# A segment mean on one core: the order of the first probe pieces and data tiles, the sizes and lead of the later pieces, and the place of the last block's counts

## The chip, the core and the metric

The kernel runs on one core of a Trainium2 chip. The core has five engines with instruction queues of their own: PE (TensorE), DVE (VectorE), ACT (ScalarE), POOL (GpSimd) and SP (SyncE, which here only issues transfers). Sixteen DMA engines move the data. The metric is the device time of one execution in microseconds (us); less is better.

## The reference

Ten million floats come with sorted segment numbers from 0 to 9999; the result is the mean of each segment.

```python
def reference(data, segment_ids):
    num_segments = int(segment_ids.max()) + 1
    sums = np.zeros(num_segments, dtype=np.float32)
    counts = np.zeros(num_segments, dtype=np.float32)
    np.add.at(sums, segment_ids, data)
    np.add.at(counts, segment_ids, 1)
    return sums / np.maximum(counts, 1)
```

The ids are drawn at random and then sorted, so a segment has about 1000 elements.

## The kernel before

Each of the 128 partitions holds 78,125 elements in a row. They are cut into 90 rows of L = 875 (the last row is shorter: 250). A row is shorter than a usual segment, so it seldom holds more than one boundary between two segments, and the kernel builds on that: for each row it needs the place of the boundary, the sum left of it and the sum of the whole row. What doesn't fit this picture is found by checks, which end in a flag (the verdict, `badi`); with the flag set, a slow general path runs at the end. With this data it doesn't run.

The steps of a row, and the names they go by:

- **Probes** (`load_probes`, L160 to L163, issued by SP): every 175th segment id, five to a row, 8 bytes each, go into `pr`. The first piece is 31 wide (rows 0 to 5), the others are 10 wide (two rows, `PIECE`), and two are 15 wide (three rows): those that begin at rows 68 and 73 (`LONG`). A piece for rows a to b also brings the first id of row b.
- **First look** (`first_look(g)`, L276 to L317, DVE): for a group of six rows, the probes tell in which block of 175 ids the boundary lies (tiles `SG`, `ST`, `far`), and where that block begins (`IDX`, `YY`). Then POOL issues six gathers.
- **Gather** (`gather`, L319, POOL): an indirect DMA per row fetches the block of ids into `GT`, a ring of 18 rows.
- **Adding the ids** (`add_ids`, L330 to L342, ACT): the sum of the block's ids, in ACT's order four to six rows ahead of the totals. From row 66 on this writes the place of the boundary, `KK`, at once; the last row's is corrected by one more instruction (L337).
- **Second look** (`second_look`, L344, DVE, rows below 66): turns six such sums into `KK`.
- **Total** (`total`, L353 to L357, ACT) and **split** (`split`, L359 to L363, DVE): the sum of a row, and the sum left of its boundary. Both read the row's half of a **data tile** (`data_t`, two rows, 875 KB; `load_data`, L167, issued by SP). There are 45 tiles in a ring of 18 buffers. Tile t holds rows 2t and 2t + 1.

Four blocks of rows (0 to 43, 44 to 61, 62 to 71, and 72 to the end) are then turned into counts (`counts`, L569: `ps`, `PS`, `ct`, `RB`), sums (`sums`, L599) and a share of the output. For the last block this is done after the last split: `sums`, `spread` and `total_of` in L830, then the output goes out. `counts(RM, R2)` needs `KK` of all rows from 72 to 89.

The order of the work is written out by hand. Each engine works through its queue in program order and waits for what an instruction needs; nothing overtakes on an engine. The main loop (L836 to L865) runs over r from -41 to 89. In each turn it issues the probe pieces and the data tiles that are due, then `add_ids`, `total(r)`, `split(r)`, and after them the steps that `put` has hung on row r (`after[r]`). The turns before r = -1 issue transfers alone. The first looks at groups 0, 1 and 2 and the second look at group 0 hang on r = -1, so on DVE they stand ahead of the first split; the later first looks hang on row 6g - 9.

When a piece or a tile is due is decided by these lines:

```python
while pnext < NR and pnext <= r + X_PIECE + (pnext > LONG[1]) + X_DATA:
    n = GROUPS[0] if pnext == 0 else PIECE + (pnext in LONG)
...
while nt < NT and 2 * nt <= r + X_DATA:
```

SP takes the transfers in this order and is not bound to the rows: it runs ahead as far as the DMA queue and the buffers let it.

Of the kernel before, what the change touches and what calls it, by code (L numbers as in the profile page):

```python
# [22 lines left out]
NR = 90  # L23
# [6 lines left out]
GROUPS = [6] * 15  # L30
X_PIECE = 15
PIECE = 2
LONG = (68, 73)
X_DATA = 26
X_LOOK = 9
RING = 18
# [7 lines left out]
R2 = NR + 4  # L44
RM = 72
# [73 lines left out]
def kernel(  # L119
# [24 lines left out]
    def x_sum(r):  # L144
        return 6 if r < HALVES else 4
# [14 lines left out]
    def load_probes(r0, r1):  # L160
        a = 0 if r0 == 0 else K * r0 + 1
        b = min(K * r1 + 1, NPR)
        nc.sync.dma_start(out=pr_flat[:, a:b], in_=ids_p[:, a * S : (b - 1) * S + 1 : S])  # L163
# [3 lines left out]
    def load_data(t):  # L167
        d = dpool.tile([P, 2 * L], FP32, name="data_t")
        a, b = 2 * t * L, min(2 * (t + 1) * L, D)
        c = b if t < NT - 1 else a + L  # L170
        nc.sync.dma_start(out=d[:, 0 : c - a], in_=data_p[:, a:c])
        if c < b:
            nc.sync.dma_start(out=d[:, c - a : b - a], in_=data_p[:, c:b])
        tiles[t] = d
# [155 lines left out]
    def add_ids(r):  # L330
        if r >= HALVES:
            nc.scalar.activation(  # L332
                out=junk_a, in_=gt32[:, r % RING, 0 : 2 * W : 2], func=ACT.Identity,
                scale=-1.0, bias=YY[:, r : r + 1], accum_out=KK[:, r : r + 1],
            )
            if r == NR - 1:
                nc.scalar.activation(out=KK[:, r : r + 1], in_=KK[:, r : r + 1], func=ACT.Identity, bias=tl)  # L337
            return
        nc.scalar.activation(  # L339
            out=junk_a, in_=gt32[:, r % RING, 0 : 2 * W : 2], func=ACT.Copy,  # L340
            accum_out=g_of(r, r + 1),
        )  # L342
# [10 lines left out]
    def total(r):  # L353
        n = min(L, D - r * L)
        d = tiles[r // 2][:, (r % 2) * L : (r % 2) * L + n]
        t = t_of(r, r + 1)
        nc.scalar.activation(out=junk_t[:, 0:n], in_=d, func=ACT.Copy, accum_out=t)  # L357

    def split(r):  # L359
        n = min(L, D - r * L)  # L360
        d = tiles[r // 2][:, (r % 2) * L : (r % 2) * L + n]
        nc.vector.scalar_tensor_tensor(  # L362
            out=junk_v[:, 0:n], in0=iota[:, 0:n], scalar=KK[:, r : r + 1], in1=d,  # L363
            op0=ALU.is_lt, op1=ALU.mult,
            accum_out=A[:, r : r + 1],
        )
# [202 lines left out]
    def counts(a, b):  # L569


        n = b - a
        ps = fpool.tile([P, n], FP32, name="ps")
        ct = fpool.tile([P, n], FP32, name="ct")

        def s1():
            nc.vector.tensor_add(out=ps, in0=KK[:, a:b], in1=QQ[:, a:b])  # L577

        def s2():
            nc.vector.tensor_tensor_scan(  # L580
                out=PS[:, a + 1 : b + 1], data0=ps, data1=ps, initial=PS[:, a : a + 1],
                op0=ALU.max, op1=ALU.max,
            )

        def s3():
            nc.vector.tensor_sub(out=ct, in0=ps, in1=PS[:, a:b])  # L586

        def s4():
            nc.vector.reciprocal(out=ct, in_=ct)  # L589

        def s5():
            c = min(b, NR)
            nc.vector.tensor_mul(out=RB[:, a:c], in0=BT[:, a:c], in1=ct[:, 0 : c - a])  # L593
            if c < b:
                nc.vector.tensor_mul(out=RB[:, c:b], in0=MX[:, 0 : b - c], in1=ct[:, c - a : n])  # L595

        return [s1, s2, s3, s4, s5]

    def sums(a, b, weigh=True):  # L599
        def s1():  # L600
            c = min(b, NR)
            nc.vector.tensor_sub(out=B[:, a:c], in0=t_of(a, c), in1=A[:, a:c])  # L602

        def s2():
            nc.vector.tensor_add(out=XX[:, a:b], in0=A[:, a:b], in1=q5[:, 4, PAD + a - 1 : PAD + b - 1])  # L605

        def s3():
            nc.vector.tensor_tensor_scan(  # L608
                out=FF[:, a:b], data0=NBP[:, a:b], data1=XX[:, a:b], initial=FFP[:, a : a + 1],
                op0=ALU.mult, op1=ALU.add,  # L610
            )

        def s4():
            nc.vector.tensor_mul(out=RF[:, PAD + a : PAD + b], in0=FF[:, a:b], in1=RB[:, a:b])

        return [s1, s2, s3, s4] if weigh else [s1, s2, s3]
# [70 lines left out]
    def place(c0, c1, t, outs):  # L687
        def s1():
            n = c1 - c0
            nc.vector.tensor_tensor(  # L690
                out=shf[:, c0:c1, 0:ND], in0=view(t[:, c0 : c0 + 1], [[1, n], [1, ND]]),
                in1=view(dm[:, 0:1], [[0, n], [1, ND]]), op=ALU.mult,
            )

        def s2():
            for a, b, d, o in outs:
                nc.vector.tensor_reduce(out=o, in_=shf[:, a:b, 0:d], axis=AX.X, op=ALU.add)

        return [s1, s2]
# [26 lines left out]
    def spread(a, b, mask, o, n, e=nc.vector):  # L726

        def s1():
            nc.vector.tensor_mul(out=RG[:, a:b], in0=FF[:, a:b], in1=RB[:, a:b])  # L729

        def s2():
            e.tensor_tensor(  # L732
                out=o, in0=mask, in1=view(RG[:, a : a + 1], [[0, n], [1, b - a]]), op=ALU.mult
            )

        return [s1, s2]

    def total_of(i, o):
        def s1():
            nc.vector.tensor_reduce(out=o, in_=i, axis=AX.X, op=ALU.add)  # L740

        return [s1]
# [17 lines left out]
    def put(r, steps, every=1):  # L760
        for i, f in enumerate(steps):
            after[r + i // every].append(f)
# [21 lines left out]
    def sentinel():  # L784
# [13 lines left out]
    p = place(CE, NO, tax, [  # L798
        (CE, T1, ND, shf[:, CE:T1, ND]), (T1, CA, ND, xa[:, T1 - C1 :, RM - R1]), (CA, NO, ND, add[:, CA - C2 :, nb])
    ])  # L800
# [25 lines left out]
    put(RM + 3, spread(R1, RM, pa[:, :, 0 : RM - R1], xa[:, :, 0 : RM - R1], CA - C1, nc.gpsimd)[1:])  # L826
    put(83, total_of(xa[:, 0 : C2 - C1, :], OUT[:, C1:C2])
        + total_of(xa[:, C2 - C1 :, :], add[:, 0 : CA - C2, nb]))
    put(NR - 5, counts(RM, R2), 99)
    put(NR - 1, sums(RM, R2, False) + spread(RM, R2, pb, add[:, :, 0:nb], NO - C2) + total_of(add, OUT[:, C2:NO]), 99)  # L830
    assert max(after) <= NR - 1

    pnext = 0
    nt = 0
    gs = 0
    for r in range(-X_PIECE - X_DATA, NR):  # L836
        while pnext < NR and pnext <= r + X_PIECE + (pnext > LONG[1]) + X_DATA:
            n = GROUPS[0] if pnext == 0 else PIECE + (pnext in LONG)
            load_probes(pnext, pnext + n)
            if pnext == 0:  # L840
                load_data(0)
                nt = 1
            pnext += n
        while nt < NT and 2 * nt <= r + X_DATA:
            load_data(nt)
            nt += 1
        if r == -X_DATA:
            nc.scalar.dma_start(
                out=snt[0 : P - 1, :],
                in_=segment_ids[D : N].rearrange("(p d) -> p d", d=D)[:, 0:1],  # L850
            )
        if r == -1:
            for f in after[r][: 5 * HEAD]:
                f()
        while r >= -1 and gs < NR and gs <= r + x_sum(gs):
            add_ids(gs)
            gs += 1
        if r == -1:
            for f in after[r][5 * HEAD :]:
                f()  # L860
        if r >= 0:
            total(r)
            split(r)
            for f in after[r]:
                f()  # L865
# [31 lines left out]
```

## Time and profile before

| | us |
|---|---|
| median of 6 runs (189.8 to 193.88) | 190.42 |
| the profiled execution, its own time | 190.5 |
| its span, from the first to the last instruction | 188.4 |
| DVE busy (74% of the span) | 138.5 |
| ACT busy (64%) | 121.0 |
| POOL busy (53%) | 100.3 |
| splits on DVE, L362: 90, mean 1.119 | 100.7 |
| totals on ACT, L357: 90, mean 0.930 | 83.7 |
| gathers on POOL, L321: 90, mean 1.007 | 90.6 |

54.62 MB went through the DMA engines, 40.50 MB in SP's queue and 14.01 MB in POOL's (the gathers). Of 70,596 packets 60,448 are under 512 bytes: the probes, most of them.

The marks: a line of the profile is "L" and a line number of the kernel. A group's line gives engine, operation, what it writes and reads, and shapes. In a list in order of time the first two figures are the start and the length, and the bracket at the end tells how long the engine stood idle before, and what ended that. In a list of waits the figures are the sum, the number and the longest. A line of a stretch gives its length, the busy time of PE, PE's weight loads, DVE, ACT and POOL with the number of instructions, the granted TensorE clock, the busy share of the DMA engines, and GB/s.

### The profile page before, as it was taken

How to read it: one execution, taken by the hardware profiler on the slowest of the kernel's cores; microseconds unless marked ns; L12 is line 12 of the kernel's file. 1: busy time of each engine (PE TensorE's matmuls, PEld its weight loads, DVE VectorE, ACT ScalarE, POOL GpSimd, SP SyncE). 2: the span in 40 equal slices, each digit the busy share in tenths (PEclk: the TensorE clock that was granted, in tenths of full speed). 3: DMA queues.
4: the chain of work that ended last, by engine and by line, in shares of the span. 5: the costliest groups of instructions: out<-in, count | busy, mean ns of one | idle time of the engine just before them, and what ended most of it. 6: DMA issues, size and time to landing. Idle time of an engine off the chain costs nothing. (4 is left out here: it accounts for less than half of the span.)

```text
span 188.4 us, 1471 instructions
## 1 busy us (share of the span) xinstructions
PE 2.2 (1%) x8; PEld 1.9 (1%) x8; DVE 138.5 (74%) x414; ACT 121.0 (64%) x371; POOL 100.3 (53%) x119
## 2 busy tenths in 40 slices
PE   0000000000002000000000000000000000010000
PEld 0000000000001000000000000000000000010000
DVE  7521394999196985757899987466889999928991
ACT  8001486864879384966809568095768794979930
POOL 4578776068734847274372745707537768781000
DMA  6899999999999999999999997999999999997000
GB/s 29 173 133 353 341 331 327 305 328 335 323 326 320 339 323 309 338 328 319 315 331 330 307 318 211 317 304 330 331 305 319 367 420 401 404 396 296 4 0 10
DMA packets 70596, 54.62 MB, mean 290 GB/s; under 512 B 60448, under 2 KB 61016, under 8 KB 70583
## 3 DMA queue, kind: packets, MB, share of 16 engines
q1 hardware_dynamic: 64651, 40.50, 73.4%
q0 software_dynamic: 5760, 14.01, 23.0%
q14 instruction: 13, 0.11, 0.2%
q10 hardware_dynamic: 172, 0.00, 0.1%
HBM read 56.59 MB, written 0.04 MB: 301 GB/s over the span
## 5 line engine op out<-in xcount | busy, mean ns | idle before, releaser
L321 POOL DMA_INDIRECT GT<-in_segment_ids_dram,IDX x90 | 90.6, 1007 | 66.8 <-ACT junk_a L339 30.7
L362 DVE SCALAR_TENSOR_TENSOR junk_v<-iota,q,data_t 128x875 bf16<-128x875 f32 x90 | 100.7, 1119 | 15.5 <-DMA data_t<-in_data_dram 12.1
L357 ACT ACTIVATE junk_t<-data_t 128x875 bf16<-128x875 f32 x90 | 83.7, 930 | 9.8 <-DMA data_t<-in_data_dram 6.6
L339 ACT ACTIVATE junk_a<-GT 128x175 f32<-128x175 int32 x66 | 22.1, 334 | 44.5 <-DMA GT<-in_segment_ids_dram,IDX 41.4
L357 ACT ACTIVATION_READ_ACCUMULATOR junk_t<-data_t 128x1 f32 x90 | 15.3, 170 | 0.0
L346 DVE SCALAR_TENSOR_TENSOR q<-YY,G 128x6 f32<-128x6 f32 x11 | 1.7, 158 | 15.4 <-issue 6.4
L332 ACT ACTIVATE junk_a<-GT,YY 128x175 f32<-128x175 int32 x24 | 9.9, 413 | 4.4 <-DMA GT<-in_segment_ids_dram,IDX 2.7
L339 ACT ACTIVATION_READ_ACCUMULATOR junk_a<-GT 128x1 f32 x66 | 9.3, 141 | 0.0
L362 DVE DVE_READ_ACCUMULATOR junk_v<-iota,q,data_t 128x1 f32 x90 | 7.4, 83 | 0.0
L285 DVE TENSOR_REDUCE SG<-pr 128x6 f32<-128x30 int32 x15 | 2.7, 180 | 5.6 <-DMA pr<-in_segment_ids_dram 5.6
L332 ACT ACTIVATION_READ_ACCUMULATOR junk_a<-GT,YY 128x1 f32 x24 | 4.6, 192 | 0.0
L294 DVE TENSOR_SCALAR far<-ST 128x6 f32<-128x6 f32 x15 | 2.7, 178 | 0.5
L187 ACT ACTIVATE GT<-q 128x3150 int32<-128x3150 f32 x1 | 3.0, 2987 | 0.0
L301 DVE SCALAR_TENSOR_TENSOR IDX<-ST,wb 128x6 int32<-128x6 f32 (+2 forms) x16 | 2.6, 165 | 0.5
L288 DVE SCALAR_TENSOR_TENSOR ST<-pr,SG 128x6 f32<-128x6 int32 x15 | 2.5, 166 | 0.5
L297 DVE TENSOR_TENSOR ST<-ST,far 128x6 f32<-128x6 f32 x15 | 2.5, 166 | 0.5
L565 DVE TENSOR_SCALAR badi<-misc 128x1 int32<-128x1 f32 x1 | 0.2, 157 | 3.1 <-PE misc L562 3.1
L722 POOL TENSOR_SCALAR pb<-pb 128x396 f32<-128x396 f32 (+1 forms) x2 | 2.3, 1141 | 0.2
L243 DVE CAST jj<-jj_i 128x128 f32<-128x128 int32 x1 | 1.5, 1511 | 0.7 <-POOL jj_i L242 0.7
L305 DVE SCALAR_TENSOR_TENSOR YY<-ST,SG 128x6 f32<-128x6 f32 x11 | 1.8, 163 | 0.0
L561 PE MATMUL misc<-bads,ones 128*128 128x1 f32 x2 | 0.6, 362 | 103.6 <-issue 103.6
L187 ACT ACT_TABLE_LOAD x1 | 1.3, 1283 | 0.7 <-PEq L881 0.7
(126 smaller groups left out, 47.5 us busy)
## 6 DMA issues: line engine op xcount, KB each, us to landing
data_t<-in_data_dram SPq DMA_DIRECT2D x44, 875.0 KB
GT<-in_segment_ids_dram,IDX POOLq DMA_INDIRECT x90
pr<-in_segment_ids_dram SPq DMA_DIRECT2D x38, 10.0 KB
data_t<-in_data_dram SPq DMA_DIRECT2D x1, 437.5 KB
data_t<-in_data_dram SPq DMA_DIRECT2D x1, 125.0 KB
out_dram<-OUT SPq DMA_DIRECT2D x1, 36.6 KB
pr<-in_segment_ids_dram SPq DMA_DIRECT2D x2, 15.0 KB
pr<-in_segment_ids_dram SPq DMA_DIRECT2D x1, 31.0 KB
```

The source lines that it names most:

```text
L187: nc.scalar.activation(out=gt32[:, :, 0 : 2 * W : 2], in_=view(q5[:, 0, 0:1], [[0, RING], [0, W]]), func=ACT.Copy)
L285: v.tensor_reduce(out=SG[:, a:b], in_=pr32[:, a:b, 0 : 2 * K : 2], axis=AX.X, op=ALU.add)
L288: v.scalar_tensor_tensor(out=ST[:, a:b], in0=VI[:, a + 1 : b + 1], scalar=float(K), in1=SG[:, a:b], op0=ALU.mult, op1=ALU.subtract,)
L294: v.tensor_scalar(out=far, in0=ST[:, a:b], scalar1=0.0, scalar2=FAR, op0=ALU.is_equal, op1=ALU.mult)
L297: v.tensor_add(out=ST[:, a:b], in0=ST[:, a:b], in1=far)
L301: v.scalar_tensor_tensor(out=IDX[:, c:d], in0=ST[:, c:d], scalar=float(w), in1=wb[:, c:d], op0=ALU.mult, op1=ALU.add)
L321: nc.gpsimd.indirect_dma_start(out=GT[:, r % RING, :], out_offset=None, in_=ids2d[:], in_offset=bass.IndirectOffsetOnAxis(ap=IDX[:, r : r ...
L332: nc.scalar.activation(out=junk_a, in_=gt32[:, r % RING, 0 : 2 * W : 2], func=ACT.Identity, scale=-1.0, bias=YY[:, r : r + 1], accum_out=K ...
L339: nc.scalar.activation(out=junk_a, in_=gt32[:, r % RING, 0 : 2 * W : 2], func=ACT.Copy, accum_out=g_of(r, r + 1),)
L357: nc.scalar.activation(out=junk_t[:, 0:n], in_=d, func=ACT.Copy, accum_out=t)
L362: nc.vector.scalar_tensor_tensor(out=junk_v[:, 0:n], in0=iota[:, 0:n], scalar=KK[:, r : r + 1], in1=d, op0=ALU.is_lt, op1=ALU.mult, accum_ ...
L722: e.tensor_scalar(out=o, in0=o, scalar1=0.0, scalar2=None, op0=ALU.is_equal)
```

## The change

Three things are changed.

1. A function, `ahead`, decides when a probe piece is due. For the pieces of rows 6 to 23 this sets data tiles between them.
2. The two long pieces are gone; all pieces but the first are two rows, and the later ones have one lead.
3. The counts of the last block hang on row 86 and not on row 85.

```diff
-LONG = (68, 73)
...
-    put(NR - 5, counts(RM, R2), 99)
+    put(NR - 4, counts(RM, R2), 99)
...
+    def ahead(p):
+        return X_PIECE if p == 0 else p - 1 - 2 * max((p - 4) // 4, (p - X_PIECE - 1) // 2)
...
-        while pnext < NR and pnext <= r + X_PIECE + (pnext > LONG[1]) + X_DATA:
-            n = GROUPS[0] if pnext == 0 else PIECE + (pnext in LONG)
+        while pnext < NR and pnext <= r + ahead(pnext) + X_DATA:
+            n = GROUPS[0] if pnext == 0 else PIECE
```

What this makes of SP's order (P6 is the piece that begins at row 6, D1 is data tile 1):

| | before | after |
|---|---|---|
| head | P0 D0 P6 P8 P10 P12 P14 P16 D1 P18 D2 P20 D3 P22 D4 P24 D5 P26 D6 | P0 D0 P6 D1 P8 P10 D2 P12 P14 D3 P16 P18 D4 P20 P22 D5 P24 P26 D6 |
| then | P28 D7 P30 D8 ... P66 D26 | the same |
| later | P68 (3 rows) D27 P71 D28 P73 (3 rows) D29 P76 D30 P78 D31 P80 D32 P82 D33 P84 D34 P86 D35 P88 D36 D37 | P68 D27 P70 D28 P72 D29 P74 D30 P76 D31 P78 D32 P80 D33 P82 D34 P84 D35 P86 D36 P88 D37 |
| end | D38 to D44 | the same |

From D6 on the same pieces stand ahead of each tile as before, up to D26. P88 is 6 wide, since no probes follow. On DVE the six instructions of the last counts come after the split of row 86, and this is the only move on DVE; the order on ACT, POOL and PE is unchanged.

## The prediction

> **What bounds the kernel now.** I read the page's slices first, then the DMA share in windows of the head, the list of waits, the order of time in the head and in the last 40 us, and last the chain.
>
> ```profile
> DVE  7521394999196985757899987466889999928991
> ...
> DMA  6899999999999999999999997999999999997000
> GB/s 29 173 133 353 341 331 327 305 328 335 323 326 320 339 323 309 338 328 319 315 331 330 307 318 211 317 304 330 331 305 319 367 420 401 404 396 296 4 0 10
> ```
>
> A slice is 4.71 us. The DMA row is at 9 from the third slice almost to 170 us: the DMA engines are full for most of the run, at some 325 GB/s while probe pieces (8-byte elements) run among the tiles and 400 GB/s and more once they are through. No engine row is as full. So up to there what arrives next decides, and the question is where the DMA engines are not full, and from which row on the engines no longer wait for them.
>
> ```profile
> 2.00:4.00 2.00, 0.00 (x0) 0.00 (x0) 1.91 (x12) 1.99 (x2) 0.56 (x5) 1.00 1.04 15
> 4.00:7.50 3.50, 0.00 (x0) 0.00 (x0) 2.66 (x18) 1.02 (x1) 2.16 (x9) 1.00 0.95 257
> 7.50:11.00 3.50, 0.00 (x0) 0.00 (x0) 0.72 (x5) 0.00 (x0) 2.06 (x2) 1.00 0.80 11
> 11.00:13.00 2.00, 0.00 (x0) 0.00 (x0) 0.60 (x4) 0.30 (x2) 1.39 (x3) 1.00 1.01 143
> 13.00:22.00 9.00, 0.00 (x0) 0.00 (x0) 0.93 (x6) 2.03 (x12) 6.87 (x8) 1.00 1.09 330
> 22.00:57.00 35.00, 0.00 (x0) 0.00 (x0) 27.27 (x62) 25.01 (x81) 19.91 (x20) 1.00 1.09 327
> ```
>
> The last two figures are DMA share and GB/s (overlapping packets make a full share read 1.04 to 1.09). Between 7.5 and 11 us, when six probe pieces stand in a row, the share is 0.80 at 11 GB/s: the only hole before 110 us. (The dip to 211 GB/s in the 25th slice, about 113 to 118 us, follows the issue of tile 27, which held SP for 6.79 us from 107.63; nothing in the change touches it, and I leave it in both.)
>
> ```profile
> DVE junk_v L362 <- DMA data_t<-in_data_dram: 12.1, 12, 2.2
> ...
> DVE SG L285 <- DMA pr<-in_segment_ids_dram: 5.6, 2, 2.9
> ...
> DVE badi L565 <- PE misc L562: 3.1, 1, 3.1
> ```
>
> The splits (L362) wait 12 times for a data tile. In order of time these waits lie between 75.7 us (row 32) and 153.57 us (row 72). Before, the rows trail the data by some us; after, DVE is dense except for one stop of 4 us at the verdict (splits of rows 80 and 81 start at 164.91 and 170.01).
>
> ```profile
> 10.45 0.18 DVE L285 TENSOR_REDUCE SG<-pr 128x6 f32<-128x30 int32 x1 [2.69 <-DMA pr<-in_segment_ids_dram]
> ...
> 14.60 0.18 DVE L285 TENSOR_REDUCE SG<-pr 128x6 f32<-128x30 int32 x1 [2.93 <-DMA pr<-in_segment_ids_dram]
> ...
> 22.02 0.16 DVE L346 SCALAR_TENSOR_TENSOR q<-YY,G 128x6 f32<-128x6 f32 x1 [6.36 <-issue]
> ...
> 31.55 0.16 DVE L346 SCALAR_TENSOR_TENSOR q<-YY,G 128x6 f32<-128x6 f32 x1 [2.32 <-ACT junk_t L357]
> ```
>
> The first looks at groups 1 and 2 wait for probes and end early; DVE then stands until the sixth gather has been added (22.02), and stands again for 2.32 us before group 1's second look.
>
> ```profile
> 153.57 1.13 DVE L362 SCALAR_TENSOR_TENSOR junk_v<-iota,q,data_t 128x875 bf16<-128x875 f32 x1 [0.26 <-DMA data_t<-in_data_dram]
> ...
> 175.75 0.29 ACT L337 ACTIVATE q<-q,tl 128x1 f32<-128x1 f32 x1
> ...
> 176.09 0.18 DVE L577 TENSOR_TENSOR ps<-q,QQ 128x22 f32<-128x22 f32 x1
> ```
>
> Row 72 is the last that waits for data. The counts of the last block start 0.05 us after ACT has made their last input (175.75 + 0.29): no wait.
>
> **The change, part by part.** Prices first. A tile is 896,000 bytes; at 413 GB/s (154 to 156 us, no probes) that is 2.17 us. A gather is 14.01 MB / 90 = 0.156 MB, 0.38 us. SP starts tile 6 at 26.94 and tile 26 at 104.41: 3.87 us for a tile, a piece and two gathers, so a piece of two rows costs 3.87 - 2.17 - 0.75 = 0.95 us.
>
> *Tiles among the first pieces.* Pieces 6 to 23 and tiles 1 to 5 change places; from tile 6 on the order is the old one, with the same bytes ahead. The gain can only be the hole. Against the 1.04 that pieces alone reach at 2 to 4 us it is (1.04 - 0.80) / 1.04 x 3.5 = 0.81 us. Against 1.09, with the two microseconds behind it, 0.93 + 0.15 = 1.08 us. Nothing is gained if pairs of pieces leave the same hole. I take 0.8 us, ends 0 and 1.1 (a loss is rival C). It reaches the end only through rows that wait for data: the waits at 75.70, 79.92, 84.25 and 87.82 (0.40, 0.76, 1.90, 1.19) are more than enough to carry it on.
>
> What becomes late is group 2's first look, which now needs pieces behind tiles 1 to 3: 14.60 + 3 x 2.17 - 0.8 + five more gathers sharing the engines (5 x 0.38 = 1.9) = 22.2 us, and its instructions end 1.07 us later (14.60 to 15.67), at 23.3. Queued behind it on DVE is the second look of group 0, now at 22.02, with all splits after it: 1.3 us late (with three more gathers and the hole at 1.1 it is 0.2). The cover is the 2.32 us stop at 31.55, where DVE waits for ACT, and ACT needs nothing of the late look. The cost is 0; without the cover it is 1.3 us at row 6, taken back by the data waits from row 32 on. Group 1's look moves behind tile 1: 10.45 + 2.17 + two gathers 0.76 = 13.4, its indices 0.9 later; the first gather that needs them starts at 16.68, because POOL issues one per 1.3 us: covered by 2.4 us less the 1.0 that the first gather took to start after its index. Group 2's gathers (24.51) need indices of about 23.2: just covered.
>
> The page "DMA: Bandwidth & Descriptors" of the Trainium skill (section "Queues, rings and completion order") says that each DMA engine goes round the queues that have work, a packet at a time; this speaks against the change, since the first gathers then take turns with 7,000-byte rows and not with small pieces. The trace shows both: the first gather, beside pieces, was issued at 8.63 and added at 12.70 (4.07 us), the sixth, beside tiles, 15.38 and 21.60 (6.22 us). By the row the sixth is slow already and the sum stays; if by the rule it lost the same 2.15 us once more, the first split would be 2.15 us late, still inside the 2.32 us.
>
> *One lead, no long pieces.* The probe elements are the same; there is one SP issue more (0.47 us, SP has room: its issues are blocked by the queue, not by work). Ahead of tiles 29 to 35 there are two rows of probes less (0.95 us), ahead of tiles 27 and 28 one row (0.48), ahead of tile 36 the last piece, of 6 elements for 10 (0.57); from tile 37 on all is as it was. Row 72 belongs to tile 36: 0.57 us, ends 0 (DVE had only 0.26 us of wait there) and 0.95. That DVE is early enough follows from the waits at rows 56 and 58 (123.47 and 128.55: 2.16 and 1.78). The last group's look (155.80) now needs a piece behind tile 36: row 72's start plus 0.57 is 154.1, covered by 1.7 us; POOL's pick of columns (147.05) needs a piece now behind tile 33, whose row 66 ran at 143.23.
>
> *Counts behind the split of row 86.* Six instructions, the same ones. There is no wait to remove (176.04 against 176.09), and their results are first used at 182.14. The cost is 0; if DVE moves up and ACT doesn't, the split of row 86 (1.17 us) now covers the difference.
>
> *Sum.* -0.8 - 0.57 = -1.4 us. After row 72 all must move along: the gathers of rows 78 on start when DVE has looked at group 13 (POOL idled 1.55 us for it before 151.22), and ACT follows them (row 78 at 158.55) up to the verdict. The profiled execution took 190.5 (span 188.4 and 2.1 around it): 189.1. The median of the runs shown is 190.42, 0.08 lower, so 189.1 stands for it too.
>
> **Rivals.** A measurement of this kernel tells about 0.5% (0.95 us) from no change: faster is below 189.47, slower above 191.37.
>
> A, the sum: 189.1, own range 188.2 to 189.4. For it: the hole, and 12 data waits that hand a shift on.
>
> B, the gain is lost in the tail. ACT, not DVE, may hold the end: it waits for the gather of row 78 from 151.22 to 158.55 (7.33 us, against 6.22 earlier), and the verdict stops DVE 4 us behind ACT. If that gather keeps its landing because tiles now press on it, DVE only stands longer at the verdict: 190.3, with 0.2 us kept. Against it: POOL waited for DVE there, so the gather starts earlier.
>
> C, the queue holds fewer small elements than this order needs. Of the six pieces one took 3.26 us to issue where the median is 0.47: it was held until the tile ahead had drained. Four times two pieces now stand ahead of a tile (8 and 10, 12 and 14, 16 and 18, 20 and 22). If the tile is let in only when they have gone, its issue (0.67 us for tile 1 at 11.03) is exposed each time: 4 x 0.67 = 2.7, less 0.57, no 0.8: 192.6. It decides from 0.34 us a pair on, where it eats the 1.4; against it, one piece per tile runs at 1.09 from 13 us on.
>
> D, the change doesn't do what it says: the two late edits are empty if rows 64 to 72 run at DVE's pace; then A loses its 0.57 and gives 189.7, within the bound of no change.
>
> **How the numbers follow.** A 0.50; B 0.18 and D 0.12, both within 0.5%, 0.30 together; C 0.20. The predicted time is A's, 189.1. The range: both upper ends of the gain, 1.1 + 0.95 = 2.05, give 188.4, less 0.5 for the scatter of the runs (189.8 is 0.6 below the median): 187.9. Above it takes in B, D and the nearer half of C: 191.6. Faster 0.50, same 0.30, slower 0.20.
>
> **What would show it.** In the profile after: DMA share of 1.0 or more in each window from 7.5 to 22 us; group 2's look near 22 to 23 us and the first split near 23.5; the second look of group 1 still near 31.5; rows 32 to 58 about 0.8 us earlier, row 72 near 152.2, the verdict near 167.7. Wrong if the share stays near 0.8 with SP held at the tiles (C), if row 72 is early and the split of row 81 still starts at 170 (B), or if rows past 32 wait for second looks instead of data.

## The result, and the profile after

The changed kernel takes 188.27 us in the median of 34 runs (187.01 to 191.87), the kernel before in the same session 189.90 us (71 runs, 188.71 to 193.88): a ratio of 0.992, with a 95% interval of 0.9904 to 0.9935, or 1.5 us. (The ratios leave out runs that lie more than 1.5% above the fastest of their kernel, and so are not quite those of the medians.) The profiled execution took 189.34 us, 1.1 above the median of its kernel; its span is 187.2 us, 1.2 below the 188.4 of before.

The slices of the page of the changed kernel, 4.68 us each:

```profile
DVE  7310099999187986756899899667679979958991
...
DMA  6999999999999999999999999999999999999000
GB/s 29 304 265 247 277 290 293 305 327 332 321 328 321 335 325 306 337 333 325 306 309 325 316 330 322 303 311 340 319 256 311 345 371 402 408 398 370 17 0 10
```

Two things differ from before. The second and third slice move 304 and 265 GB/s instead of 173 and 133: the head has tiles in it now. And the dip of before, 211 GB/s in the 25th slice, is gone. The stretches of the head (DMA share and GB/s at the end of each line) and of 110 to 120 us, the changed kernel:

```profile
7.50:11.00 3.50, 0.00 (x0) 0.00 (x0) 0.00 (x0) 0.00 (x0) 2.78 (x3) 1.00 1.20 270
11.00:13.00 2.00, 0.00 (x0) 0.00 (x0) 0.35 (x3) 0.00 (x0) 1.44 (x2) 1.00 1.14 256
13.00:22.00 9.00, 0.00 (x0) 0.00 (x0) 0.57 (x4) 3.63 (x16) 6.98 (x7) 1.00 1.08 287
...
110.00:120.00 10.00, 0.00 (x0) 0.00 (x0) 9.21 (x26) 7.46 (x24) 4.53 (x5) 1.00 1.11 317
```

The share is over 1.0 throughout. But 13 to 22 us, at 330 GB/s before, is down to 287: the pieces that made the hole now run there. The waits of DVE that were shown of before, now of the changed kernel:

```profile
DVE SG L284 <- DMA pr<-in_segment_ids_dram: 15.5, 2, 9.6
...
DVE junk_v L361 <- DMA data_t<-in_data_dram: 12.1, 12, 1.7
...
DVE badi L564 <- issue: 1.2, 1, 1.2
```

The first looks wait 15.5 us instead of 5.6; the splits wait for tiles as long as before, 12.1 us; the stop at the verdict has shrunk from 3.1 to 1.2 us. In order of time, DVE of the changed kernel (start, length, and in brackets the idle time before):

```profile
12.58 0.18 DVE L284 TENSOR_REDUCE SG<-pr 128x6 f32<-128x30 int32 x1 [5.83 <-DMA pr<-in_segment_ids_dram]
...
23.29 0.18 DVE L284 TENSOR_REDUCE SG<-pr 128x6 f32<-128x30 int32 x1 [9.65 <-DMA pr<-in_segment_ids_dram]
...
31.38 0.16 DVE L345 SCALAR_TENSOR_TENSOR q<-YY,G 128x6 f32<-128x6 f32 x1
...
153.70 1.13 DVE L361 SCALAR_TENSOR_TENSOR junk_v<-iota,q,data_t 128x875 bf16<-128x875 f32 x1 [0.85 <-DMA data_t<-in_data_dram]
...
176.10 0.18 DVE L576 TENSOR_TENSOR ps<-q,QQ 128x22 f32<-128x22 f32 x1
```

The look at group 2 is 8.7 us later than before and the first split (24.45) 2.24 us later, yet the second look of group 1 (31.38 for 31.55) is not late: the stop of 2.32 us has gone. Row 72 starts at 153.70, no earlier than the 153.57 of before, after a wait of 0.85 us instead of 0.26. The gain of 1.2 us in this pair of executions therefore shows only after row 72: the verdict moved from 169.11 to 167.90.

### The profile page after: what moved, and what is told of

Read it like the earlier page. It is cut to its first block, busy times and chain, and to the rows that moved or that the text cites. A ratio compares the mean times of both kernels' runs of the same rounds, so it can differ in the third digit from the quotient of the medians.

```text
span 187.2 us, 1472 instructions
## 1 busy us (share of the span) xinstructions
PE 2.2 (1%) x8; PEld 1.9 (1%) x8; DVE 137.2 (73%) x414; ACT 121.0 (65%) x371; POOL 100.0 (53%) x119
## 5 line engine op out<-in xcount | busy, mean ns | idle before, releaser
L361 DVE SCALAR_TENSOR_TENSOR junk_v<-iota,q,data_t 128x875 bf16<-128x875 f32 x90 | 100.7, 1118 | 16.2 <-DMA data_t<-in_data_dram 12.1
L284 DVE TENSOR_REDUCE SG<-pr 128x6 f32<-128x30 int32 x15 | 2.7, 178 | 15.5 <-DMA pr<-in_segment_ids_dram 15.5
L720 POOL TENSOR_TENSOR pb<-KL,jj 128x396 f32<-128x396 f32 (+1 forms) x2 | 1.6, 808 | 0.2
L560 PEld LDWEIGHTS misc<-bads,ones 128*128 128x128 f32 x2 | 0.5, 310 | 103.7 <-issue 103.7
```

What stands on the lines that cost most here:

```text
L284: v.tensor_reduce(out=SG[:, a:b], in_=pr32[:, a:b, 0 : 2 * K : 2], axis=AX.X, op=ALU.add)
L361: nc.vector.scalar_tensor_tensor(out=junk_v[:, 0:n], in0=iota[:, 0:n], scalar=KK[:, r : r + 1], in1=d, op0=ALU.is_lt, op1=ALU.mult, accum_ ...
```

## The experiments

Twelve runs were made in three further sessions (the changed kernel once more, and the head alone twice), each beside its own runs of the kernel before, whose median was 188.14, 188.42 and 190.06 us. Times are compared inside a session only.

### The three parts one by one (kernel before: 188.14)

The head alone (the old rule for pieces past row 26):

```diff
+    def ahead(p):
+        if p == 0 or p > 26:
+            return X_PIECE + (p > LONG[1])
+        return p - 1 - 2 * max((p - 4) // 4, (p - X_PIECE - 1) // 2)
```

> Only the head of the change: tiles 1 to 5 among the pieces of rows 6 to 26, long pieces and counts as before. Theory P (the prediction's): the hole in the DMA share at 7.5 to 11 us is filled and tile 6 and all after it come 0.8 us earlier; the time falls by 0.8 us, ratio 0.996. Theory Q (from the trace after): a piece costs about 0.95 us wherever it stands (six in a row took from 7.2 to 13 us), so the hole was none; tile 6 is issued and landed as before within 0.3 us and the time is the same, ratio 1.000 within 0.002. Theory C (queue too shallow for pairs of pieces): slower, 1.005 or more.

The later pieces alone (the old rule up to row 26, no long pieces):

```diff
+        if p <= 26:
+            return X_PIECE
+        return p - 1 - 2 * max((p - 4) // 4, (p - X_PIECE - 1) // 2)
```

> Only the later pieces: none of three rows, one lead, head and counts as before. P: tiles 29 to 36 come 0.57 to 0.95 us earlier, the time falls by 0.57 us, ratio 0.997. Q: the same on ACT (the gather of row 78 about 0.5 us earlier, the verdict with it), but DVE then reaches the last counts before ACT has their input, so that a part of it is lost at the counts: between 0.997 and 1.000, and DVE waits 0.3 us or more before the counts' first instruction. If the pieces do nothing: 1.000 and the split of row 66 not earlier than 143.2.

The counts alone:

```diff
-    put(NR - 5, counts(RM, R2), 99)
+    put(NR - 4, counts(RM, R2), 99)
```

> Only the last block's counts behind the split of row 86. P and Q: no wait to remove (input ready at 176.04, counts at 176.09), ratio 1.000 within 0.001. If the counts usually wait for ACT and the profiled execution was an exception: down to 0.997.

And the changed kernel with the counts put back behind row 85:

> The change without its third part: counts behind the split of row 85 again. P (third part worth nothing): the change's own ratio, 0.992. Q: in the trace after, the split of row 85 ends at 174.96 and ACT has the last input at 175.39, so the counts here wait 0.45 us and the time is 0.45 us over the change's: ratio 0.9945.

| kernel | median, us | ratio | 95% interval | row 72 starts, us |
|---|---|---|---|---|
| head alone | 187.45 | 0.9962 | 0.9927 to 0.9997 | 152.54 |
| later pieces alone | 187.87 | 0.9996 | 0.9955 to 1.0036 | 153.38 |
| counts alone | 188.41 | 1.0009 | 0.9977 to 1.0040 | 153.15 |
| head and later pieces | 188.22 | 0.9968 | 0.9924 to 1.0012 | 153.67 |

Only the head alone is clear of no change, by 0.7 us, close to the 0.8 of its step; tile 6 lands at 36.57 and 36.63 in the two kernels with the head and at 37.10 and 37.59 in the two without, as its theory P had it. The third batch comes back to both. The wait of 0.3 us or more ahead of the last counts, which theory Q expected in the later pieces alone and in head and later pieces, is in neither. The later pieces alone win nothing, though their rows run ahead: row 70 starts at 149.92, against 150.32 with the counts alone. Then the lead is lost; with the later pieces row 72 waits 0.93 us for its tile, with the head alone 0.41:

```profile
153.38 1.13 DVE L362 SCALAR_TENSOR_TENSOR junk_v<-iota,q,data_t 128x875 bf16<-128x875 f32 x1 [0.93 <-DMA data_t<-in_data_dram]
```

```profile
152.54 1.13 DVE L362 SCALAR_TENSOR_TENSOR junk_v<-iota,q,data_t 128x875 bf16<-128x875 f32 x1 [0.41 <-DMA data_t<-in_data_dram]
```

Why the rows run ahead is seen at 110 to 120 us, first the head alone, then the later pieces alone:

```profile
110.00:120.00 10.00, 0.00 (x0) 0.00 (x0) 7.16 (x20) 6.63 (x22) 5.37 (x6) 1.00 0.93 258
```

```profile
110.00:120.00 10.00, 0.00 (x0) 0.00 (x0) 8.37 (x24) 7.35 (x24) 5.12 (x6) 1.00 1.08 340
```

The long piece of rows 68 to 70 stands ahead of tile 27, and while it is moved few tile bytes are. Over all fourteen profiled executions this splits cleanly: 258 to 292 GB/s in the seven with the long pieces, 309 to 341 in the seven without.

### What gives the lead back at tile 36 (kernel before: 188.42)

The changed kernel once more, then head and counts without the later pieces:

> The changed kernel itself, beside the next three on one chip. Theory H (the head alone carries the gain; the two-row pieces give back at tile 36 what they win before it): the same time as head and counts without the pieces, within 0.4 us, about 187.3 where the kernel before stands at 188.2; row 72 starts near 153.4 with 0.7 to 1.0 us of wait, row 80 waits about 0.7 us for its tile, the stretch from 150 to 155 us moves 360 to 380 GB/s. Rival (the terms add up, as the prediction had it): 0.5 us or more below head and counts.

> Head and counts, the old pieces with the two long ones. Theory H: 0.7 us below the kernel before, ratio 0.996, and not above the changed kernel by more than 0.4 us; row 72 near 152.5 without a wait of over 0.3 us, tile 36 lands 0.3 to 0.5 us earlier than in the changed kernel, 150 to 155 us moves 410 GB/s. Rival (the terms add up): 0.5 us above the changed kernel, ratio 0.996 against 0.993.

The changed kernel with its last piece ahead of tile 36, beside the piece of rows 86 and 87:

```diff
-        return X_PIECE if p == 0 else p - 1 - 2 * max((p - 4) // 4, (p - X_PIECE - 1) // 2)
+        return X_PIECE if p == 0 else p - 1 - 2 * max((p - 4) // 4, (p - X_PIECE - 1) // 2) + 2 * (p == 88)
```

> The changed kernel with its last piece one tile earlier, ahead of tile 36 as in the kernel before. If that piece's new place is what gives the gain back: tiles 37 to 40 land 0.5 to 0.8 us earlier than in the changed kernel, row 80's wait of 0.69 us goes, the time falls by 0.3 to 0.7 us below it. Rival (the bytes ahead decide, wherever the piece stands, and the rows that run earlier bring their gathers earlier too): the landings of tiles 37 to 40 and the time stay within 0.3 us of the changed kernel's.

The kernel before with only its last piece moved behind tile 36:

```diff
-        while pnext < NR and pnext <= r + X_PIECE + (pnext > LONG[1]) + X_DATA:
+        while pnext < NR and pnext <= r + X_PIECE + (pnext > LONG[1]) - 2 * (pnext == 88) + X_DATA:
```

> The kernel before with one edit alone, its last piece (6 elements) moved from ahead of tile 36 to behind it. Theory H, if the piece's place costs: tile 36 no earlier than in the kernel before by more than 0.3 us, tiles 37 to 40 0.4 to 0.8 us later, time 0 to 0.7 us above. Rival, the prediction's pricing: tile 36 lands 0.57 us earlier, tile 37 and all later ones as before, time 0 to 0.5 us below.

| kernel | median, us | ratio | 95% interval |
|---|---|---|---|
| the changed kernel | 187.78 | 0.9972 | 0.9951 to 0.9994 |
| head and counts | 188.49 | 1.0014 | 0.9983 to 1.0044 |
| changed, last piece early | 188.90 | 1.0048 | 1.0021 to 1.0076 |
| before, last piece late | 188.65 | 1.0026 | 0.9994 to 1.0057 |

Three of the four expectations of theory H failed. Head and counts were not the whole of the gain here: the changed kernel is 0.7 us better, as "the terms add up" said. Putting the last piece early did not return a loss, and did not leave things as they were either; it made a loss of 1.1 us. The fourth held: moving the piece late in the old kernel brings tile 36 no earlier (by the count of rows explained below 152.32, with head and counts 151.89) and tiles 37 to 40 0.7 to 0.9 us later than there, where the prediction's pricing had 0.57 us to gain. Two reservations: head and counts has another head, since the kernel before has no profile beside it, and the time, 1.0026, is not clear of no change. The changed kernel's gain is 0.3% here and 0.8% in the first session, with intervals that don't meet; the stop of ACT, below, bears on that.

The kernel with the last piece early shows what two pieces side by side do late in the run. Its stretch of 145 to 150 us, and SP's queue (start and length; "x2" are the two pieces, 4.65 us to issue):

```profile
145.00:150.00 5.00, 0.00 (x0) 0.00 (x0) 4.83 (x16) 3.71 (x11) 3.23 (x5) 1.00 0.87 195
```

```profile
140.80 4.65 SPq L162 DMA_DIRECT2D pr<-in_segment_ids_dram  x2
145.55 4.58 SPq L170 DMA_DIRECT2D data_t<-in_data_dram  x4
```

The changed kernel in the same stretch:

```profile
145.00:150.00 5.00, 0.00 (x0) 0.00 (x0) 4.74 (x16) 3.24 (x9) 3.23 (x5) 1.00 1.06 310
```

195 GB/s instead of 310: SP was held at the second piece, and no tile followed until 145.55. This is what rival C was afraid of, at a place where it was not looked for. That it costs the 1.1 us is not shown. This execution took 187.70 us, the shortest of the twelve, and the profiled changed kernel 188.44. By the count of rows tiles 36 to 40 are 1.0 to 1.7 us later here, but the splits that wait for them start earlier: row 72 at 152.88 for 153.08, row 80 at 164.80 for 165.37 (it still waits 0.69 us), much as the first theory had it for tiles 37 to 40. So the profile has a gain of the size that this theory expected, and the median a loss; what the loss comes from is open.

### A longer hole, a later look, and the parts that were missing (kernel before: 190.06)

The head alone again, and later pieces and counts without the head:

> The head alone once more, on whatever chip this is, beside a kernel without the head and one with a longer hole. Theory H (the hole at 7.5 to 11 us is worth 0.7 to 0.8 us of the end): ratio 0.994 to 0.998 of the kernel before, tiles 8 to 24 land 0.4 to 1.0 us earlier than in the next kernel, which has no head. Rival (the head gives nothing that lasts, as head with counts on the second chip had it, 1.0014): 0.999 to 1.002.

> The later pieces and the counts, with the old head. Theory H: ratio 0.998 to 1.002, DMA share of 0.75 to 0.95 from 7.5 to 11 us as before; no dip from 112 to 117 us, since the three-row piece ahead of it is gone, and tiles 27 to 29 1.5 to 2.5 us earlier than in the head alone, of which 0.3 us or less is left at tile 36. Rival (the later pieces are what gains): 0.996 or less, and tile 36 0.5 us earlier than in the head alone.

The kernel before with a longer hole, eleven pieces in a row where it had six:

```diff
-        while pnext < NR and pnext <= r + X_PIECE + (pnext > LONG[1]) + X_DATA:
+        while pnext < NR and pnext <= r + X_PIECE + (pnext > LONG[1]) + 11 * (pnext <= 26) + X_DATA:
```

> The kernel before with the hole made longer: all eleven pieces of rows 6 to 27 in a row ahead of tile 1, where before it was six. Theory H, the hole's price grows with the pieces in a row: six cost 0.8 us, eleven 1.5, so 0.7 us slower, ratio 1.002 to 1.007; tile 6 lands 0.5 to 1.0 us later than in the kernel before, and rows 32 to 56 start as much later. Rival (whatever stands in the head, rows of 32 and later are fed at the same pace and the end stays): 0.999 to 1.001.

The changed kernel with the head's pieces a tile later still:

```diff
-max((p - 4) // 4, (p - X_PIECE - 1) // 2)
+max(min((p - 4) // 4 + 1, 5), (p - X_PIECE - 1) // 2)
```

> The changed kernel with the pieces of the head one tile later still: tiles 0 and 1 first, then piece 6, tile 2, pieces 8 and 10, and so on. The second group's look gets later by a tile and its gathers, to 25.5 to 27 us, and the first split to 26.5 to 28, 4.5 to 6 us later than in the kernel before, which is more than the 2.32 us stop covers. Theory (the splits up to row 32 are not what the end hangs on; the waits for data from row 32 on take any lateness of up to their sum of some 8 us): row 6 is 2 to 3.5 us late, row 48 on time within 0.5 us, and the time within 0.4 us of the changed kernel's, ratio 0.995 to 0.999. Rival (a late first look goes through to the end): 2 us or more above, 1.008 and up.

| kernel | median, us | ratio | 95% interval | tile 6, us | tile 22, us |
|---|---|---|---|---|---|
| head alone | 188.97 | 0.9959 | 0.9928 to 0.9990 | 37.69 | 98.19 |
| later pieces and counts | 189.06 | 0.9955 | 0.9923 to 0.9987 | 37.68 | 98.35 |
| longer hole | 189.81 | 0.9999 | 0.9970 to 1.0028 | 37.73 | 98.42 |
| pieces a tile later | 188.86 | 0.9954 | 0.9915 to 0.9993 | 37.45 | 99.06 |

(The last two columns, and every landing of a tile in this document that is not called recorded, are counts: tile t has landed when 128 x (t + 1) rows of 7,000 bytes have arrived. In the eight executions whose trace records the landing of tile 36 itself, it is 0.6 to 2.1 us later, and 33 to 113 rows of the tiles behind it have come by then. The last piece early is the 0.6; so two single executions can't be told apart by the count where they differ by a microsecond or so.)

The longer hole cost nothing that shows (0.5 us at most, by its interval): "the price grows with the pieces in a row" has fallen, and its rival held. It moves 202 GB/s at 13 to 22 us, where the kernel before moved 330, and makes up for it with 357 at 22 to 57, for 327:

```profile
13.00:22.00 9.00, 0.00 (x0) 0.00 (x0) 3.35 (x11) 3.03 (x15) 6.87 (x8) 1.00 1.00 202
22.00:57.00 35.00, 0.00 (x0) 0.00 (x0) 24.88 (x59) 25.62 (x82) 19.92 (x20) 1.00 1.06 357
```

In these four tile 6 lands within 0.3 us whatever the order ahead of it; the same pieces have to be moved before it in all of them. Nor is the hole the same from one execution to the next: in the five with the old head the share at 7.5 to 11 us is 0.76 to 0.99, and later pieces and counts has the 0.99. So the low share there was for the most part not lost time but the price of the pieces, paid at one place. The head alone gained 0.4% once more, but not by the tiles of the middle: at tiles 8 to 24 it is at most 0.2 us ahead of later pieces and counts, where 0.4 to 1.0 us was expected.

Later pieces and counts, which theory H held to be worth nothing, gained as much as the head: the rival's 0.996 or less held, and its tile 36 (151.17) is the 0.5 us ahead of the head alone (151.66). Its tiles 27 to 29 come 1.0 to 1.5 us earlier, less than the 1.5 to 2.5 expected. The next section says what the counts' place has to do with it.

The later look was harmless to the time, as the theory said. DVE of the kernel with the pieces a tile later:

```profile
26.64 0.18 DVE L284 TENSOR_REDUCE SG<-pr 128x6 f32<-128x30 int32 x1 [8.29 <-DMA pr<-in_segment_ids_dram]
...
27.81 1.13 DVE L361 SCALAR_TENSOR_TENSOR junk_v<-iota,q,data_t 128x875 bf16<-128x875 f32 x1
...
34.73 0.16 DVE L345 SCALAR_TENSOR_TENSOR q<-YY,G 128x6 f32<-128x6 f32 x1
```

The first split is 5.6 us and row 6 3.2 us later than before, more than the 2.32 us stop covers. The splits' waits for tiles fall from 12.1 to 8.9 us and take part of it. It was not all taken by row 48 (108.89, 0.5 to 1.0 us later than in the other three), as the expectation had it, nor by row 72 (154.26 for 153.02 to 153.26); this was one of the longer executions, 189.98 us where the median is 188.86. The kernel's ratio, 0.9954, lies between the two of the changed kernel, 0.992 and 0.9972.

### The stop of ACT, and what the counts' place is worth

Around 167 us ACT stands still in some executions with nothing to wait for. First the changed kernel in the first session, then the same kernel in the session at 188.42 (ACT, start and length):

```profile
166.64 0.15 ACT L356 ACTIVATION_READ_ACCUMULATOR junk_t<-data_t 128x1 f32 x1
167.97 0.42 ACT L331 ACTIVATE junk_a<-GT,YY 128x175 f32<-128x175 int32 x1 [1.18 <-ACT junk_t L356]
```

```profile
165.70 0.16 ACT L356 ACTIVATION_READ_ACCUMULATOR junk_t<-data_t 128x1 f32 x1
165.81 0.42 ACT L331 ACTIVATE junk_a<-GT,YY 128x175 f32<-128x175 int32 x1
```

The stop is 0.82 to 1.77 us long in all six executions profiled in the two sessions where the kernel before took 190 us, and absent from all eight in the two where it took 188 (one has a wait of 0.67 us there, for DVE, and one stands for 0.2). It makes `KK` late, and with the counts behind row 85 DVE waits for it, 1.85 us in the kernel with the longer hole and 0.45 in the head alone of that session, though not in the kernel before of the first session, where the verdict had held DVE as long. With the counts behind row 86 it doesn't, as in later pieces and counts. First DVE of the longer hole, then of later pieces and counts:

```profile
173.69 0.08 DVE L362 DVE_READ_ACCUMULATOR junk_v<-iota,q,data_t 128x1 f32 x1
175.63 0.18 DVE L577 TENSOR_TENSOR ps<-q,QQ 128x22 f32<-128x22 f32 x1 [1.85 <-ACT q L337]
```

```profile
174.06 1.13 DVE L362 SCALAR_TENSOR_TENSOR junk_v<-iota,q,data_t 128x875 bf16<-128x875 f32 x1 [0.45 <-ACT junk_a L332]
175.12 0.08 DVE L362 DVE_READ_ACCUMULATOR junk_v<-iota,q,data_t 128x1 f32 x1
175.29 0.18 DVE L577 TENSOR_TENSOR ps<-q,QQ 128x22 f32<-128x22 f32 x1
```

In the second the split of row 86 fills the time up to `KK` (ACT's last correction ran from 174.96 to 175.25). By these traces the counts' new place is worth 0 to 1.1 us, the length of that split, when ACT stops; no run times it alone in such a session. Without the stop it is worth nothing, as the counts alone showed (1.0009). That the stop makes the two 190 us sessions slower is read from the traces, not shown by a run that takes it away. The trace has an instruction packet of 8,192 bytes just ahead of it (166.47 to 166.78 us before, 165.87 to 166.19 after), but the executions without a stop have one as well (164.19 to 164.50 in the changed kernel's second profile). What holds ACT is open. It need not be the chip: the sessions at 188.42 and 190.06 both ran on chip number 3.

## Why the prediction was right, and which steps were not

The sign and the size are right: 189.1 was forecast for a kernel that stood at 190.42, and the ratio of 0.992 makes 188.9 of it. The sum of -1.4 us is met by 1.5. The way there is not the one forecast, so that the sizes meet is luck; in the session at 188.42 the same change gave 0.5 us.

**Where the lead goes.** For twelve of the fourteen profiled executions (all but the two with new orders of the changed kernel) the landing of a tile was fitted by least squares with one number for each of the three edits (the longer hole and the late last piece counted as the kernel before). In us, with standard errors; negative is earlier:

| tile | the head | the later pieces |
|---|---|---|
| 6 | -0.27 ± 0.20 | -0.25 ± 0.21 |
| 8 | -0.90 ± 0.29 | -0.22 ± 0.30 |
| 22 | -0.82 ± 0.37 | 0.20 ± 0.38 |
| 28 | -0.66 ± 0.26 | -1.46 ± 0.27 |
| 30 | -0.49 ± 0.24 | -1.36 ± 0.25 |
| 34 | -0.08 ± 0.26 | -0.82 ± 0.28 |
| 36 | -0.24 ± 0.20 | -0.20 ± 0.21 |
| 40 | -0.12 ± 0.24 | 0.14 ± 0.25 |

Both leads are there in the middle of the run and are gone by tile 36; row 72 starts 0.10 ± 0.24 us earlier with the head and 0.13 ± 0.25 later with the new pieces, and row 80 0.75 ± 0.27 later with these. Counting packets says why the leads end. In the eight executions whose trace records the landing of tile 36 itself (152.42 in the head alone of the session at 188.14, 153.25 in the later pieces alone, 152.96 in the changed kernel's second profile), by that moment all 57,216 probe elements have come, the last piece's among them though it stands behind tile 36 with the new pieces, and 4,992 packets of gathers, exactly those of 78 rows: row 78's own gather is only issued at 150.75 in the changed kernel, after the look at its group. Ahead of it the account is open. At tile 34, by the count, the kernels with the new pieces have had 54,895 to 55,088 probe elements and the others 56,101 to 56,236: about 1,130 fewer, which at the prediction's price (0.95 us for 1,280) is 0.84 us, the whole lead of 0.82. And a kernel whose rows run ahead has used its lead to gather earlier: at tile 35 4,913 to 4,985 gather packets have come with the new pieces and 4,850 to 4,914 with the old ones. At tile 36 the account is closed: but for the 33 to 113 rows of later tiles the same bytes are through, in whatever order, and what is left of a lead there is 0.2 us for either edit, no more than its error.

**The head, -0.8.** As a lead at tiles 8 to 28 it has about the size forecast (0.7 to 0.9 in the table, 0.4 at tiles 12 and 16). That "the gain can only be the hole" was wrong: the longer hole cost nothing that shows, and at tile 6, the first with the same pieces ahead in both orders, the lead is 0.27 us. It appears by tile 8, where the kernels with the head have had 83 gather packets fewer on the mean (1,196 for 1,279), 0.5 us at 0.38 us for the 64 of a gather: part of the lead is gathers that come later. Nor does it reach the end through the waits of rows 32 to 56, as the step had it; at tile 36 0.2 us of it is left. What does reach the end goes by the path that the prediction named for the time after row 72, the gather of row 78 and ACT behind it. DVE's look at that group follows row 69, where a lead is still there (row 70: 0.32 ± 0.23 us with the head). By the same fit the head has this gather issued 0.50 ± 0.23 us earlier, row 78 added 0.70 ± 0.32 and ACT's last sum for the verdict made 0.60 ± 0.31 earlier; with the new pieces the first two are 0.37 ± 0.25 and 0.10 ± 0.34 us earlier, the third 0.04 ± 0.32 later. What the head has here is two standard errors, no more, but it agrees with the 0.4% of the two sessions with the head alone (0.7 and 0.8 us by their ratios).

**The later pieces, -0.57 at row 72.** This is the term that was mis-sized: it is about 0 there, and row 72 waits 0.85 us where 0.26 was seen. The step priced tile 36 by "the last piece, of 6 elements for 10", as if a piece behind a tile in SP's order came after it. It was all through when tile 36 landed, in all eight executions that record it. And the prediction looked at the dip at 113 to 118 us, wrote that "nothing in the change touches it" and left it in both. It was the long piece ahead of tile 27, and taking it out is worth 1.5 us at tile 28, three times what the step gave it; only it doesn't last either.

**The counts, 0.** Right without ACT's stop. The step's second half, "if DVE moves up and ACT doesn't, the split of row 86 (1.17 us) now covers the difference", is what happened in the session of the result: in the changed kernel the split of row 85 ended at 174.95 and `KK` was there at 175.39, so that the counts at the old place would have waited 0.44 us.

**The late looks, 0.** Right, and tested with a look 3.4 us later still. The first split was late by 2.24 us and not by 1.3, since the look itself was at 23.29; the 2.32 us stop just covered it. The Trainium skill's rule that the prediction weighed (page "DMA: Bandwidth & Descriptors", section "Queues, rings and completion order": each DMA engine goes round the queues that have work) was there read as a sixth gather 2.15 us later. That did not come: the sixth gather was added 5.01 us after its issue, for 6.22 before, and the split waited for the look. The first gather, now beside a tile, took 5.41 us for 4.07. How the engines take turns is not shown by this.

**The verdict.** 167.7 was forecast and 167.90 measured, but by another road: not through row 72 at 152.2 (it was 153.70), but through a stop that shrank from 3.06 to 1.17 us. ACT had the verdict's last sum 0.5 us earlier (165.48 for 165.99), and PE took it up 1.8 us after that instead of 2.5. PE before, then after (the bracket names a total of ACT; what the line reads is that sum):

```profile
168.49 0.58 PE L562 MATMUL misc<-bads,ones 128*128 128x1 f32 x2 [3.46 <-ACT junk_t L357]
```

```profile
167.27 0.59 PE L561 MATMUL misc<-bads,ones 128*128 128x1 f32 x2 [2.74 <-ACT junk_t L356]
```

These 0.7 us are not the change's. PE follows the sum within 0.1 us in all eight executions of the two sessions at 188 us, and after 0.05 to 2.5 us in the six of the two at 190. Its lateness comes in the sessions of ACT's stop but is not the stop itself: in later pieces and counts ACT stopped for 1.21 us and PE followed at once. So 0.7 of the 1.2 us of this pair is chance, and the 167.7 was hit by it. The 1.2 us are kept to the end (the last output is issued 1.16 us earlier); at their old place the counts would have waited for 0.44 us of them.

Rival B, a loss in the tail, is thus half true: the lead in the data is lost, at tile 36 already, but the gather of row 78, which it feared would keep its landing, was added 0.97 us earlier (157.58 for 158.55). Rival C did not occur in the changed kernel (two pieces ahead of a tile in the head cost nothing that reaches the end); at 141 us two pieces do hold SP, and what that costs is open. Rival D, "the two late edits are empty", is right for row 72 and wrong for the rows ahead of it.

What stays open: how the 1.5 us of the first session divide among the three edits. The single parts gave 0 to 0.4%, with intervals of 0.3 to 0.4% to either side, and the combinations do not add up inside them (the head alone 0.996 twice, with the counts 1.0014). The changed kernel itself gave 0.8% and 0.3%, and no run takes ACT's stop or PE's lateness away.

## What to carry to other kernels

Where every transfer up to some point must be through before the next stage can start, a change of order ahead of that point gives the rows in between a lead, and the lead is spent there on transfers that would have come anyway; price a reorder at the point where the same bytes are through in both orders, and ask what was started on the way while the lead lasted (here the gather of row 78). A low share or few GB/s while small elements run is their price, not a hole to be filled, until a run that makes it longer shows that it costs. An instruction that needs another engine's last result can stand one long instruction later at no cost (1.0009 here), and then covers a stop of that engine. And one profile of a kernel whose times scatter by 1% may be of an execution that doesn't show what the median shows: look where it stands among the others first.

## What the runs showed of the hardware

- A piece of 1,920 8-byte elements (rows 68 to 70) ahead of a tile brings 110 to 120 us down to 258 to 292 GB/s from 309 to 341; two pieces side by side at 141 us held SP for 4.65 us and brought 145 to 150 us to 195 (one execution).
- A transfer that SP issued behind a tile can be through when the tile lands: all 768 elements of the last piece, issued at 146.99, have come by 152.96, when tile 36, issued ahead of it at 141.98, lands (the changed kernel's second profile).
- ACT stood still for 0.82 to 1.77 us at 167 us in six executions of six in two sessions, and in none of eight in two others (over 0.2 us with nothing to wait for); the changed kernel and the head alone are in both groups. In the same six PE took up ACT's sum 0.05 to 2.5 us after it was made, in the eight within 0.1.
